# A four-layer diffusion trunk on one core: adaLN chunks spread anew over the stages, and five smaller reorderings

## The chip, the cores and the metric

One Trainium2 chip, one core. The kernel is one launch; its time is the device time of that launch in microseconds, the median of several runs. Every large matrix product is made of three terms of fp32r operands (a value is split in a high and a low part; high x high, high x low and low x high are added up in PSUM).

## The reference, cut to what matters

128 context tokens and 256 latent tokens, 1024 features, four layers. Layer i has the mixer i mod 3: 0 is a gated MLP (gMLP), 1 a pooling mixer, 2 an attention. Each layer ends with a gated convolutional FFN.

```python
def run_trunk(x, cond, is_context, cache_k, cache_v, weights):
    for i in range(DEPTH):                       # 4
        kind, j = i % N_MIXERS, i // N_MIXERS
        sh1, sc1, gt1, sh2, sc2, gt2 = ada_params(cond, w_ada[i], b_ada[i])   # silu(cond) @ w + b
        h = rms_norm(x, g_mix[i]) * (1 + sc1) + sh1
        y = ...                                  # chunk_gmlp, multi_pool or attention
        x = x + gt1 * y
        h = rms_norm(x, g_ffn[i]) * (1 + sc2) + sh2
        x = x + gt2 * conv_ffn(h, w_ffn_in[i], ffn_conv_w[i], ffn_conv_b[i], w_ffn_out[i])

def conv_ffn(h, w_in, conv_w, conv_b, w_out):
    a, u = jnp.split(h @ w_in, 2, axis=-1)       # 2 x 2816
    ap = jnp.pad(a, ((0, 0), (1, 1), (0, 0)))
    a = ap[:, :-2] * conv_w[0] + ap[:, 1:-1] * conv_w[1] + ap[:, 2:] * conv_w[2] + conv_b
    return (jax.nn.gelu(a) * u) @ w_out
```

## The kernel before, in words

**Layout.** Activations lie transposed: 8 tiles (d) of 128 features by 384 tokens in `x`. A product takes a 128x128 block of weights against 384 tokens. Matmuls of the FFN, of the gate half of the gMLP and of the output projections are issued by `mm3` (line 688), those of the first half of the gMLP on line 862, of the pool on line 1030.

**Weights.** All weights come through one stream of 582 chunks, nearly all of 512 KB, in the order of `chunk_plan`, which weaves the adaLN chunks of the table `ADA` into each stage's weights; `EDGES` holds how many weights lead and how many rest. SP issues the loads in that order into five buffers `wraw`; a load waits until the buffer of an earlier chunk is free. A weight chunk is split by ScalarE (`whi`, line 349) and VectorE (`wlo`, line 356) ahead of its use, up to four `wsp` buffers.

**adaLN.** The shift, scale and gate of a layer (six types of 8 chunks each: mixer shift 0, scale 1, gate 2; FFN shift 3, scale 4, gate 5) are products of the conditioning vectors with their own chunks. A chunk "ad" goes to VectorE, `ada_dve`, line 391: two multiply-accumulates, one for each conditioning vector. A chunk "ap" goes to TensorE, `ada_pe`, line 409: eight instruction records in a bank of the pool `psa`; after eight chunks a row copy on ScalarE and, some chunks later, two transposes on TensorE (`ada_fin`). Layer 0's first two types are chunks "a0", two per feature tile, worked on in the start (`a0_mm`, `a0_fin`, `a0_put`), where a hook called after each feature tile's first pass of the first gMLP block finishes tile k+1's scale and shift, norms it, and issues tile k+2's adaLN products. The entries of `ADA` name the layer and stage: gv and gu (first and second half of the gMLP's input), go (its output), fi and fo (FFN input and output), nm, qkv, at (attention's norm, projections and core).

**FFN.** `prep` gives a function `after(d)` that runs behind the residual of tile d (line 464): it scales `x` into `hh` (ScalarE, line 624) and `hl` (VectorE, line 626), and squares x (line 477) into the sum `acc` (line 479; the last square is added later, line 484). The FFN has 22 tiles f, each with a gate half `pa` and a value half `pu`, 48 matmuls a tile. The first `NR` tiles use `hh`, `hl`, which are not yet divided by the rms: these products have two more columns for the shift (386 in all), and their epilogue multiplies by the reciprocal rms (lines 714 to 719). The later tiles use normed inputs, which `put_one` makes in eight steps during tiles 0 to 2, alternately in two forms: for even k, VectorE multiplies (line 585), ScalarE scales (587) and rounds to the high part (588), VectorE subtracts (589); for odd k, VectorE scales and multiplies (592), ScalarE adds the shift into the high part (594), VectorE subtracts (598). Each piece of lines 587, 592, 594 and 598 runs once for the context and once for the latent tokens. PSUM: six banks in the ring `mm`, one in `px` (statistics, transposes), one in `psa`.

**Statistics.** `stats` (line 536) sums `acc`, and a second part where one is given, over the features with matmuls against ones. The pool gives it both `acc` and the last square.

Of the kernel before, what the change touches and what calls it, by code (L numbers as in the profile page):

```python
# [36 lines left out]
NR = 3  # L37
# [243 lines left out]
class Prog:  # L281
# [188 lines left out]
    def square(self, d, acc):  # L470
# [7 lines left out]
        if d < KD - 1:  # L478
            nc.vector.tensor_tensor(out=acc, in0=acc, in1=sq, op=ALU.add)
        return sq  # L480

    def add_square(self, pr):

        self.nc.vector.tensor_tensor(out=pr["acc"], in0=pr["acc"], in1=pr["sq"], op=ALU.add)
# [95 lines left out]
    def put_one(self, k, A, rbs, hi, lo, sh, act):  # L580
# [3 lines left out]
        if act:  # L584
            nc.vector.tensor_tensor(out=t, in0=self.x[:, k, :], in1=rbs, op=ALU.mult)
            for c, (t0, t1) in enumerate(GRPS):
                nc.scalar.activation(t[:, t0:t1], t[:, t0:t1], AF.Identity, scale=A[:, k, c:c + 1], bias=sh[:, k, c:c + 1])
            nc.scalar.activation(hi[:, k, :], t, AF.Copy)
            return lambda: nc.vector.tensor_tensor(out=lo[:, k, :], in0=t, in1=hi[:, k, :].bitcast(F32),
                                                   op=ALU.subtract)  # L590
        for c, (t0, t1) in enumerate(GRPS):
            nc.vector.scalar_tensor_tensor(out=t[:, t0:t1], in0=self.x[:, k, t0:t1], scalar=A[:, k, c:c + 1],
                                           in1=rbs[:, t0:t1], op0=ALU.mult, op1=ALU.mult)
            nc.scalar.activation(hi[:, k, t0:t1], t[:, t0:t1], AF.Identity, bias=sh[:, k, c:c + 1])

        def last():
            for c, (t0, t1) in enumerate(GRPS):
                nc.vector.scalar_tensor_tensor(out=lo[:, k, t0:t1], in0=t[:, t0:t1], scalar=sh[:, k, c:c + 1],
                                               in1=hi[:, k, t0:t1].bitcast(F32), op0=ALU.add, op1=ALU.subtract)
# [1100 lines left out]
```

## Time and profile before

| | us |
|---|---|
| median of 3 runs (lowest to highest) | 1788.74 (1787.39 to 1789.23) |
| the profiled execution's own time | 1788.39 |
| its span, from first to last instruction | 1786.6 |
| mean granted clock of TensorE, of full speed | 0.996 |
| busy: TensorE / VectorE / ScalarE | 1754.6 / 1371.8 / 872.2 |

The profile is one execution. TensorE's busy time counts matmuls whose ends are modelled, weight loads (PEld) overlap them. A line names the source line of the kernel before; the arrow in "out<-in" points from inputs to output. Stages, in us from the span's start: the start to 15, gMLP of layer 0 to 261 with its output stage from about 190, the FFN of layer 0 to 534, pool and FFN of layer 1 to 854 with the output stage from 754, attention from 924 to 971 within layer 2, and the last layer's gMLP and FFN to the end.

### The profile page before, as it was taken

How to read it: one execution, taken by the hardware profiler on the slowest of the kernel's cores; microseconds unless marked ns; L12 is line 12 of the kernel's file. 1: busy time of each engine (PE TensorE's matmuls, PEld its weight loads, DVE VectorE, ACT ScalarE, POOL GpSimd, SP SyncE). 2: the span in 40 equal slices, each digit the busy share in tenths (PEclk: the TensorE clock that was granted, in tenths of full speed). 3: DMA queues.
4: the chain of work that ended last, by engine and by line, in shares of the span. 5: the costliest groups of instructions: out<-in, count | busy, mean ns of one | idle time of the engine just before them, and what ended most of it. 6: DMA issues, size and time to landing. Idle time of an engine off the chain costs nothing.

```text
span 1786.6 us, 26835 instructions
## 1 busy us (share of the span) xinstructions
PE 1754.6 (98%) x10230; PEld 1675.2 (94%) x10230; DVE 1371.8 (77%) x2369; ACT 872.2 (49%) x1635; POOL 1.8 (0%) x30
## 2 busy tenths in 40 slices
PE   9999989999999999999998999999999999999999
PEld 7799889999998899998777999999988999999999
DVE  5888688888986888899687788887775767876632
ACT  3644236545455654432469565453454434755521
POOL 0000000000000000000000000000000000000000
PEclk9999999999999999999999999999999999999999
DMA  8764663555663355567550335655546344354341
GB/s 323 280 222 147 234 211 130 189 191 198 219 212 106 126 181 200 200 214 241 203 183 1 131 130 188 197 176 202 193 150 204 112 145 145 123 175 151 136 150 57
DMA packets 87636, 311.64 MB, mean 174 GB/s; under 512 B 10450, under 2 KB 10962, under 8 KB 87252
## 3 DMA queue, kind: packets, MB, share of 16 engines
q1 hardware_dynamic: 87220, 309.92, 50.9%
q8 instruction: 80, 1.31, 0.3%
q14 instruction: 48, 0.39, 0.1%
q10 hardware_dynamic: 288, 0.01, 0.0%
HBM read 308.06 MB, written 1.84 MB: 173 GB/s over the span
## 4 chain that ended last, share of the span: by engine, by line
PE 61%; DVE 22%; ACT 8%; issue 5%; DMA 4%; SPq 0%; DVEq 0%; ACTq 0%
PE mm L688 45%; DVE wlo L356 7%; DVE junk L391 7%; PE mm L862 6%; DMA wraw<-wts 4%; ACT whi L349 3%; DVE ct L736 3%; PE S L688 1%; PE mm L906 1%; ACT gg L745 1%; DVE gl L606 1%; PE adaT L688 1%; PE S L1138 1%; PE adaT L862 1%; PE psa L862 1%
## 5 line engine op out<-in xcount | busy, mean ns | idle before, releaser
L688 PE MATMUL mm<-hb,whi 128*128 128x384 f32 (+1 forms) x4064 | 888.7, 338 | 6.6 <-ACT whi L349 2.6
L688 PEld LDWEIGHTS mm<-hb,whi 128*128 128x128 f32 x4064 | 722.7, 189 | 11.6 <-ACT whi L349 3.3
L356 DVE TENSOR_TENSOR wlo<-wraw,whi 128x1024 fp32r<-128x1024 f32 (+2 forms) x390 | 466.3, 1201 | 213.7 <-ACT whi L349 212.4
L349 ACT ACTIVATE whi<-wraw 128x1024 fp32r<-128x1024 f32 (+2 forms) x390 | 399.3, 1034 | 270.3 <-PE mm L688 139.4
L688 PE MATMUL mm<-hb,wlo 128*128 128x384 f32 (+1 forms) x2032 | 521.4, 337 | 0.8 <-DVE wlo L356 0.8
L391 DVE SCALAR_TENSOR_TENSOR junk<-wraw,condb 128x1024 bf16<-128x1024 f32 x304 | 371.6, 1222 | 9.1 <-ACT condb L1618 2.7
L688 PEld LDWEIGHTS mm<-hb,wlo 128*128 128x128 f32 x2032 | 369.1, 189 | 1.3 <-DVE wlo L356 1.3
L745 ACT ACTIVATE gg<-ct 128x128 f32<-128x128 f32 (+1 forms) x152 | 47.0, 357 | 248.9 <-DVE ct L736 248.9
L688 PE MATMUL mm<-gh,whi 128*128 128x384 f32 x448 | 123.9, 338 | 3.2 <-ACT whi L349 3.2
L688 PE MATMUL mm<-gh,wlo 128*128 128x384 f32 x448 | 124.2, 338 | 2.4 <-DVE wlo L356 2.4
L688 PE MATMUL mm<-gl,whi 128*128 128x384 f32 x448 | 123.8, 338 | 0.0
L736 DVE SCALAR_TENSOR_TENSOR ct<-ab,par,ct 128x385 f32<-128x385 f32 x176 | 108.7, 619 | 6.4 <-ACT ct L734 2.7
L624 ACT ACTIVATE hb<-x,A 128x128 fp32r<-128x128 f32 x96 | 43.2, 457 | 103.9 <-DVE x L464 93.1
L862 PE MATMUL mm<-whi,hb 128*128 128x512 f32 x320 | 87.6, 399 | 0.0
L688 PEld LDWEIGHTS mm<-gh,whi 128*128 128x128 f32 x448 | 81.9, 189 | 4.1 <-ACT whi L349 4.1
L688 PEld LDWEIGHTS mm<-gh,wlo 128*128 128x128 f32 x448 | 82.0, 189 | 3.6 <-DVE wlo L356 3.6
L688 PEld LDWEIGHTS mm<-gl,whi 128*128 128x128 f32 x448 | 82.3, 189 | 0.0
L746 DVE TENSOR_TENSOR gg<-mm,gg 128x384 f32<-128x384 f32 x76 | 42.4, 558 | 47.4 <-ACT gg L745 46.7
L862 PEld LDWEIGHTS mm<-whi,hb 128*128 128x128 f32 x320 | 60.8, 190 | 15.6 <-ACT hb L573 0.4
L734 ACT ACTIVATE ct<-ab,par 128x385 f32<-128x385 f32 x88 | 62.7, 713 | 3.4
L464 DVE SCALAR_TENSOR_TENSOR x<-mm,prm,x 128x128 f32<-128x128 f32 x92 | 33.6, 411 | 22.9 <-PE mm L688 22.7
L862 PE MATMUL mm<-wlo,hb 128*128 128x512 f32 x160 | 47.8, 405 | 0.0
(286 smaller groups left out, 1651.8 us busy)
## 6 DMA issues: line engine op xcount, KB each, us to landing
wraw<-wts SPq DMA_DIRECT2D x562, 512.0 KB, 3.9
wraw<-wts SPq DMA_DIRECT2D x12, 256.0 KB, 2.6
wraw<-wts SPq DMA_DIRECT2D x8, 384.0 KB, 4.1
x<-x SPq DMA_DIRECT2D x4, 384.0 KB, 4.5
mx<-mix SPq DMA_DIRECT2D x1, 1280.0 KB, 7.8
y<-x SPq DMA_DIRECT2D x3, 384.0 KB, 3.1
condb<-condb SPq DMA_DIRECT2D x1, 1024.0 KB, 7.1
ws<-a_w_s SPq DMA_DIRECT2D x2, 512.0 KB, 4.3
```

The lines of the kernel that those rows point to most:

```text
L349: nc.scalar.activation(hi[:, :n], t[:, :n], AF.Copy)
L356: nc.vector.tensor_tensor(out=lo[:, :n], in0=t[:, :n], in1=hi[:, :n].bitcast(F32), op=ALU.subtract)
L391: nc.vector.scalar_tensor_tensor(out=self.junk.bitcast(BF16), in0=w, scalar=1.0, in1=self.condb[:, c, :], op0=ALU.mult, op1=ALU.mult, accu ...
L464: nc.vector.scalar_tensor_tensor(out=x[:, d, t0:t1], in0=ps[:, t0:t1], scalar=self.prm[:, l, ty * 8 + d, c:c + 1], in1=x[:, d, t0:t1], op0 ...
L606: nc.vector.tensor_tensor(out=lo, in0=src, in1=hi.bitcast(F32), op=ALU.subtract)
L624: nc.scalar.activation(self.hh[:, d, t0:t1], self.x[:, d, t0:t1], AF.Copy, scale=A[:, d, c:c + 1])
L688: nc.tensor.matmul(o, w[:, c:c + nw], r, start=(first and p == 0), stop=(last and p == 2))
L734: nc.scalar.activation(t, ab[:, 1:T + 2], AF.Identity, scale=cw[1], bias=cb)
L736: nc.vector.scalar_tensor_tensor(out=t, in0=ab[:, i:i + T + 1], scalar=cw[i], in1=t, op0=ALU.mult, op1=ALU.add)
L745: nc.scalar.activation(g[:, t0:t1], t[:, t0 + c:t1 + c], GELU)
L746: nc.vector.tensor_tensor(out=g, in0=u, in1=g, op=ALU.mult)
L862: nc.tensor.matmul(ps[n][i], hs, w[p == 1][:, c:c + 512], start=(k == 0 and p == 0), stop=(k == 7 and p == 2))
```

## The change

- `ADA`: the gate half of layer 0's gMLP takes 12 chunks on VectorE instead of 10, its output 9 instead of 12, the input stage of its FFN 19 instead of 18; the input stage of layer 1's FFN 16 instead of 18, its output stage 16 instead of 22. Layer 2's type (2, 3), the FFN's shift, is no longer in layer 1 but goes to TensorE within attention, ahead of (2, 5). Chunks on VectorE are 144 instead of 152, on TensorE 32 instead of 24. In the plan, attention's stage then has ten adaLN chunks, the first two chunks of the output projection, and six adaLN chunks; before, two, the two, and six.
- `NR` is per layer: in layer 1 tile 3 is unnormed too.
- Tile 3 of every FFN takes its two banks from `psa` and `px` instead of the ring.
- `put_one` uses the even form for all eight steps.
- `after(7)` squares first and adds that square to `acc`, ahead of the scaling; the separate additions (lines 773 and 934) go, and the pool's statistic has one part.
- The hook of the first block is called after pass 0 (finish and norm of tile k+1) and again after pass 1 (adaLN products of tile k+2, and the load of `condb`).

```diff
--- before.py
+++ after.py
@@ -34,7 +34,7 @@
 CW = 1024
 TE = T + 2
 
-NR = 3
+NR = (3, 4, 3, 3)
 
 NG = NF - 8
 
@@ -46,15 +46,15 @@
 
 ADA = {
     (0, "gv"): [("ad", 0, 4)],
-    (0, "gu"): [("ad", 0, 2), ("ad", 0, 3, 0, 2)],
-    (0, "go"): [("ad", 0, 3, 2, 8), ("ad", 0, 5, 0, 6), ("ap", 1, 1)],
-    (0, "fi"): [("ad", 0, 5, 6, 8), ("ad", 1, 2), ("ad", 1, 0)],
+    (0, "gu"): [("ad", 0, 2), ("ad", 0, 3, 0, 4)],
+    (0, "go"): [("ad", 0, 3, 4, 8), ("ad", 0, 5, 0, 5), ("ap", 1, 1)],
+    (0, "fi"): [("ad", 0, 5, 5, 8), ("ad", 1, 2), ("ad", 1, 0)],
     (0, "fo"): [("ad", 1, 4), ("ad", 1, 3)],
-    (1, "fi"): [("ad", 1, 5), ("ad", 2, 1), ("ad", 2, 0, 0, 2)],
-    (1, "fo"): [("ad", 2, 0, 2, 8), ("ad", 2, 4), ("ad", 2, 3)],
+    (1, "fi"): [("ad", 1, 5), ("ad", 2, 1)],
+    (1, "fo"): [("ad", 2, 0), ("ad", 2, 4)],
     (2, "nm"): [("ap", 2, 2, 0, 6)],
     (2, "qkv"): [("ap", 2, 2, 6, 8)],
-    (2, "at"): [("ap", 2, 5)],
+    (2, "at"): [("ap", 2, 3), ("ap", 2, 5)],
     (2, "fi"): [("ad", 3, 1), ("ad", 3, 2)],
     (2, "fo"): [("ad", 3, 0), ("ad", 3, 4, 0, 4)],
     (3, "gv"): [("ad", 3, 4, 4, 8), ("ad", 3, 3, 0, 4)],
@@ -467,7 +467,7 @@
         if after is not None:
             after(d)
 
-    def square(self, d, acc):
+    def square(self, d, acc, joined=False):
 
         nc = self.nc
         if d == 0:
@@ -475,13 +475,9 @@
             return None
         sq = self.tmp.tile([128, T], F32, tag="sq", name="sq")
         nc.scalar.activation(sq, self.x[:, d, :], AF.Square)
-        if d < KD - 1:
+        if d < KD - 1 or joined:
             nc.vector.tensor_tensor(out=acc, in0=acc, in1=sq, op=ALU.add)
         return sq
-
-    def add_square(self, pr):
-
-        self.nc.vector.tensor_tensor(out=pr["acc"], in0=pr["acc"], in1=pr["sq"], op=ALU.add)
 
     def new_acc(self):
         return self.tmp.tile([128, T], F32, tag="acc", name="acc", bufs=1)
@@ -577,28 +573,15 @@
                                                scalar=self.prm[:, l, k, c:c + 1], in1=hi[:, k, t0:t1].bitcast(F32),
                                                op0=ALU.add, op1=ALU.subtract)
 
-    def put_one(self, k, A, rbs, hi, lo, sh, act):
+    def put_one(self, k, A, rbs, hi, lo, sh):
 
         nc = self.nc
         t = self.tmp.tile([128, T], F32, tag="sq", name="nt")
-        if act:
-            nc.vector.tensor_tensor(out=t, in0=self.x[:, k, :], in1=rbs, op=ALU.mult)
-            for c, (t0, t1) in enumerate(GRPS):
-                nc.scalar.activation(t[:, t0:t1], t[:, t0:t1], AF.Identity, scale=A[:, k, c:c + 1], bias=sh[:, k, c:c + 1])
-            nc.scalar.activation(hi[:, k, :], t, AF.Copy)
-            return lambda: nc.vector.tensor_tensor(out=lo[:, k, :], in0=t, in1=hi[:, k, :].bitcast(F32),
-                                                   op=ALU.subtract)
+        nc.vector.tensor_tensor(out=t, in0=self.x[:, k, :], in1=rbs, op=ALU.mult)
         for c, (t0, t1) in enumerate(GRPS):
-            nc.vector.scalar_tensor_tensor(out=t[:, t0:t1], in0=self.x[:, k, t0:t1], scalar=A[:, k, c:c + 1],
-                                           in1=rbs[:, t0:t1], op0=ALU.mult, op1=ALU.mult)
-            nc.scalar.activation(hi[:, k, t0:t1], t[:, t0:t1], AF.Identity, bias=sh[:, k, c:c + 1])
-
-        def last():
-            for c, (t0, t1) in enumerate(GRPS):
-                nc.vector.scalar_tensor_tensor(out=lo[:, k, t0:t1], in0=t[:, t0:t1], scalar=sh[:, k, c:c + 1],
-                                               in1=hi[:, k, t0:t1].bitcast(F32), op0=ALU.add, op1=ALU.subtract)
-
-        return last
+            nc.scalar.activation(t[:, t0:t1], t[:, t0:t1], AF.Identity, scale=A[:, k, c:c + 1], bias=sh[:, k, c:c + 1])
+        nc.scalar.activation(hi[:, k, :], t, AF.Copy)
+        return lambda: nc.vector.tensor_tensor(out=lo[:, k, :], in0=t, in1=hi[:, k, :].bitcast(F32), op=ALU.subtract)
 
     def split_act(self, src, hi, lo):
         nc = self.nc
@@ -620,13 +603,16 @@
                 nc.vector.tensor_copy(self.hh[:, :, T:TE], sh)
                 nc.vector.tensor_tensor(out=self.hl[:, :, T:TE], in0=sh, in1=self.hh[:, :, T:TE].bitcast(F32),
                                         op=ALU.subtract)
+            if d == KD - 1:
+                self.square(d, res["acc"], True)
             for c, (t0, t1) in enumerate(GRPS):
                 nc.scalar.activation(self.hh[:, d, t0:t1], self.x[:, d, t0:t1], AF.Copy, scale=A[:, d, c:c + 1])
             for c, (t0, t1) in enumerate(GRPS):
                 nc.vector.scalar_tensor_tensor(out=self.hl[:, d, t0:t1], in0=self.x[:, d, t0:t1],
                                                scalar=A[:, d, c:c + 1], in1=self.hh[:, d, t0:t1].bitcast(F32),
                                                op0=ALU.mult, op1=ALU.subtract)
-            res["sq"] = self.square(d, res["acc"])
+            if d < KD - 1:
+                self.square(d, res["acc"])
             if extra is not None:
                 extra(d)
 
...
@@ -757,7 +743,7 @@
 
                 last = None
                 for k in range(KD):
-                    this = self.put_one(k, pr["A"], rbs, nh, nl, sh, k % 2 == 0)
+                    this = self.put_one(k, pr["A"], rbs, nh, nl, sh)
                     if last is not None:
                         last()
                     last = this
@@ -770,7 +756,6 @@
                 for _ in range(n):
                     next(steps, None)
 
-            self.add_square(pr)
             b = [self.bank()[:, :TE] for _ in range(4)]
             R = None
             for kk in range(4):
@@ -789,8 +774,9 @@
 
             prev = [(0, b[0], b[1]), (1, b[2], b[3])]
             for f in range(2, NF):
-                w0 = TE if f < NR else T
-                pa, pu = self.bank()[:, :w0], self.bank()[:, :w0]
+                w0 = TE if f < NR[l] else T
+
+                pa, pu = (p()[:, :w0] for p in ((self.ps_bank, self.px_bank) if f == 3 else (self.bank, self.bank)))
                 now, prev = (prev, []) if f == 5 else (prev[:1], prev[1:])
                 for kk in range(2):
                     if kk == 0:
@@ -802,11 +788,11 @@
                         w = self.w_get("fi")
                         for st, g in zip(sts, gs):
                             self.split_act(g, gh[st[0]], gl[st[0]])
-                    if f < NR:
+                    if f < NR[l]:
                         norm(3)
                     for k4 in range(4):
                         k = 4 * kk + k4
-                        r = (hh[:, k, :], hl[:, k, :]) if f < NR else (nh[:, k, :], nl[:, k, :])
+                        r = (hh[:, k, :], hl[:, k, :]) if f < NR[l] else (nh[:, k, :], nl[:, k, :])
                         self.mm3([(pa, 256 * k4), (pu, 256 * k4 + 128)], w, r, k == 0, k == 7)
                 prev.append((f, pa, pu))
             assert next(steps, 0) == 0 and len(prev) == 1
@@ -861,8 +847,8 @@
                             hs = (vl if p == 2 else vh)[:, k, 128 * i:128 * i + 128]
                             nc.tensor.matmul(ps[n][i], hs, w[p == 1][:, c:c + 512],
                                              start=(k == 0 and p == 0), stop=(k == 7 and p == 2))
-                    if p == 0 and hook is not None and len(cs) == 2:
-                        hook(k)
+                    if p < 2 and hook is not None and len(cs) == 2:
+                        hook[p](k)
 
             def vout(b, ps):
                 for i in range(3):
@@ -931,7 +917,6 @@
                 vout(1, ps[1])
                 b0, m0 = 2, 0
             else:
-                self.add_square(pr)
                 b = [self.bank()[:, :TE] for _ in range(4)]
                 rbs = None
 
@@ -1060,7 +1045,7 @@
                     aft(d)
 
             first(0)
-            r = self.stats(pr["acc"], pr["sq"])
+            r = self.stats(pr["acc"])
             first(1)
             scaled(0)
             first(2)
@@ -1605,10 +1590,12 @@
         a0_mm(1)
         nc.sync.dma_start(self.cst[:, 0:512], a["cst"][:, 0:512])
 
-        def hook(k):
+        def hook0(k):
             if k + 1 < KD:
                 a0_put(k + 1, a0_fin(k + 1))
-                a0_mm(k + 2)
+
+        def hook1(k):
+            a0_mm(k + 2)
             if k == 3:
                 nc.sync.dma_start(self.condb, a["condb"].rearrange("p (c d) -> p c d", c=2))
             if k == 7:
@@ -1623,7 +1610,7 @@
             kind, j = l % 3, l // 3
             prep = lambda l=l: self.prep(l, 1)
             if l == 0:
-                pr = self.gmlp(l, j, prep, None, hook)
+                pr = self.gmlp(l, j, prep, None, (hook0, hook1))
             elif kind == 0:
                 pr = self.gmlp(l, j, prep, pr)
             elif kind == 1:
```

## Rows read from the trace of the kernel before

**Rows 1.** Page, part 1: busy us (share of the span) and instructions of each engine.
```profile
PE 1754.6 (98%) x10230; PEld 1675.2 (94%) x10230; DVE 1371.8 (77%) x2369; ACT 872.2 (49%) x1635; POOL 1.8 (0%) x30
```

**Rows 2.** Waits of TensorE by releaser, whole span: us in total, times, longest.
```profile
PE mm L688 <- ACT whi L349: 5.7, 4, 2.6
...
PE mm L688 <- DVE wlo L356: 3.2, 5, 0.8
...
PE psa L1550 <- DMA wraw<-wts: 2.7, 3, 1.7
...
PE mm L688 <- DVE hb L589: 2.3, 1, 2.3
...
PE cs L536 <- DVE acc L484: 2.1, 1, 2.1
...
PE mm L688 <- ACT ab L732: 1.0, 2, 0.6
...
PE Tps L1210 <- ACT kd L1205: 0.8, 1, 0.8
```

**Rows 3.** Busy us by stretch: PE, PEld, DVE, ACT, POOL, clock, DMA share, GB/s.
```profile
21.40:24.90 3.50, 3.50 (x10) 2.76 (x9) 1.23 (x1) 1.06 (x1) 0.00 (x0) 0.51 1.04 408
...
247.50:253.50 6.00, 6.00 (x19) 6.00 (x20) 5.90 (x11) 0.00 (x0) 0.00 (x0) 0.50 0.54 183
...
442.50:534.40 91.90, 91.59 (x528) 91.27 (x528) 81.46 (x136) 42.49 (x71) 0.00 (x0) 1.00 0.63 212
...
590.80:620.80 30.00, 26.42 (x147) 24.94 (x145) 24.32 (x43) 18.81 (x38) 0.00 (x0) 1.00 0.33 117
...
754.00:853.90 99.90, 94.64 (x532) 92.54 (x534) 87.68 (x140) 29.61 (x41) 0.00 (x0) 0.98 0.69 234
```

**Rows 4.** Page, parts 5 and 6: groups of instructions; weight chunks with us to landing.
```profile
L356 DVE TENSOR_TENSOR wlo<-wraw,whi 128x1024 fp32r<-128x1024 f32 (+2 forms) x390 | 466.3, 1201 | 213.7 <-ACT whi L349 212.4
...
L391 DVE SCALAR_TENSOR_TENSOR junk<-wraw,condb 128x1024 bf16<-128x1024 f32 x304 | 371.6, 1222 | 9.1 <-ACT condb L1618 2.7
...
wraw<-wts SPq DMA_DIRECT2D x562, 512.0 KB, 3.9
```

**Rows 5.** Timeline of VectorE, gMLP output of layer 0: start, us.
```profile
240.12 1.22 DVE L391 SCALAR_TENSOR_TENSOR junk<-wraw,condb 128x1024 bf16<-128x1024 f32 x1
...
241.27 0.74 DVE L464 SCALAR_TENSOR_TENSOR x<-mm,prm,x 128x128 f32<-128x128 f32 x2
```

**Rows 6.** One line's instructions, lines 409 and 536: ns min/median/max, first and last start.
```profile
L409 PE MATMUL psa<-wraw,cond x192: 379/379/403, 176.9 to 933.4; 128*32 128x256 f32 x192
...
L536 PE MATMUL cs<-ones,sq x12: 250/250/250, 537.4 to 856.5; 128*128 128x1 f32 x12
```

**Rows 7.** Busy time of line 409 alone, end of layer 1.
```profile
853.84:855.27 1.43, 1.43 (x24) 0.67 (x24) 1.00 0.05 19
```

**Rows 8.** Busy time by stretch, attention; the last of three such steps stands.
```profile
938.31:952.09 13.78, 11.28 (x99) 9.65 (x98) 11.20 (x44) 11.22 (x35) 0.00 (x0) 1.00 0.01 2
...
964.77:971.14 6.37, 5.90 (x58) 5.36 (x59) 5.46 (x22) 5.91 (x21) 0.00 (x0) 1.00 0.01 3
```

**Rows 9.** One line's instructions, the norm's lines 585 to 594: ns min/median/max.
```profile
L585 DVE TENSOR_TENSOR nt<-x,rbs x16: 550/556/561, 268.3 to 1528.7; 128x384 f32<-128x384 f32 x16
...
L587 ACT ACTIVATE nt<-nt,prm,A x32: 493/542/590, 268.9 to 1529.7; 128x128 f32<-128x128 f32 x16, 128x256 f32<-128x256 f32 x16
...
L588 ACT ACTIVATE hb<-nt x16: 524/526/527, 269.9 to 1530.3; 128x384 fp32r<-128x384 f32 x16
...
L592 DVE SCALAR_TENSOR_TENSOR nt<-x,A,rbs x32: 345/416/481, 268.8 to 1530.2; 128x128 f32<-128x128 f32 x16, 128x256 f32<-128x256 f32 x16
...
L594 ACT ACTIVATE hb<-nt,prm x32: 384/447/508, 270.4 to 1531.1; 128x128 fp32r<-128x128 f32 x16, 128x256 fp32r<-128x256 f32 x16
```

**Rows 10.** Timelines of VectorE and TensorE, first FFN: last low part, last input used.
```profile
285.75 0.74 DVE L598 SCALAR_TENSOR_TENSOR hb<-nt,prm,hb 128x128 fp32r<-128x128 f32 x2
...
291.10 0.51 PE L688 MATMUL mm<-hb,wlo 128*128 128x384 f32 x2
```

More of the change, by code (lines that the diff above doesn't have):

```diff
@@ L710, in epi_a @@
             def epi_a(f, pa, pu):
-                if f >= NR:
+                if f >= NR[l]:
                     return f, pa, None, pu, None
@@ L742, in epi_c @@
                 g = self.tmp.tile([128, T], F32, tag="gg", name="gg")
-                if f >= NR:
+                if f >= NR[l]:
                     for c, (t0, t1) in enumerate(GRPS):
@@ L804, in ffn @@
                             self.split_act(g, gh[st[0]], gl[st[0]])
-                    if f < NR:
+                    if f < NR[l]:
                         norm(3)
```

## Prediction

> **What bounds the kernel now.** I read the page's engine line first [rows 1]. TensorE is busy for 1754.6 of 1786.6 us, so all its gaps together are 32.0 us; VectorE, busy 1371.8 us, is next. Outside the gaps and the half-clock stretches no faster VectorE or ScalarE can move the end. The reader is to look for two things: where TensorE waits, and where its clock is granted at half.
>
> The waits of TensorE by releaser [rows 2] name few places: a split's high part from ScalarE (5.7 us), its low part from VectorE (3.2), a DMA (2.7), one normed tile (2.3) and the sum of squares (2.1). Then I cut the trace into stages [rows 3]. The pace to compare with is the FFN output stage of layer 0: 528 matmuls in 91.59 busy us, 0.1735 us each. The same stage of layer 1 takes 99.90 us for 532. The remaining windows show half clock (0.50, the 1.2 GHz level) behind the waits, and this nearly doubles what a short wait costs: 247.5 to 253.5 passes 19 matmuls in 6.00 us, which at 0.1735 would be 3.3, so 2.7 us are lost on top of the wait that stands before it.
>
> **The change, part by part.** *Fewer adaLN chunks on VectorE in layer 1's output stage.* A chunk there is two multiply-accumulates of 1.222 us [rows 4], 2.44 us of VectorE, and a split's low part costs 1.20. The stage goes from 22 chunks to 16, which is exactly what layer 0's stage carries. VectorE falls by 6 x 2.44 = 14.7 us, from 87.68 to about 73 of some 92 us; layer 0's is at 81.46 and TensorE is idle there for 91.90 - 91.59 = 0.3 us [rows 3]. Gain: 99.90 - 91.90 - 4 x 0.1735 = 7.3 us; I take 7.2, and 4 to 7.6 as ends (the low end if the wait at the join from the FFN's first half, followed by half clock, survives).
>
> *Second FFN with four unnormed tiles.* In layer 1's FFN TensorE stops once, for 2.3 us, for the normed input that VectorE finishes by line 589 [rows 2]. With tile 3 unnormed the first normed product comes one tile, 48 matmuls, 8.3 us, later; the wait has 6 us to spare. The rest of that stretch holds smaller stops on tiles' epilogues, one on line 732 that keeps a PSUM bank of the ring. The stretch of 30.00 us holds 147 matmuls [rows 3], 25.5 us at pace: 4.5 lost. Tile 3's banks leave the ring, so the bank that line 732 holds is no longer the next one wanted. Added work is two columns of 386 on TensorE and three short VectorE operations. I take 4.4, ends 3.3 and 4.6. The same bank wait elsewhere is half of the row "ab L732" in [rows 2]: another 0.5 us.
>
> *gMLP output and FFN start of layer 0.* VectorE runs four multiply-accumulates of adaLN back to back, the last at 240.12, and only then the residual of output tile 2 at 241.27 [rows 5]; that tile's scaling and square on ScalarE, and the split that TensorE wants next, are queued behind this residual. TensorE's 2.6 us wait for that split, 0.8 for its low part, the 2.7 us of half clock, and 2.1 for the sum of squares add to 8.2 us. The change takes two adaLN chunks away before this residual (4.9 us of VectorE) and one behind it, and puts the last square ahead of the last scaled tile, so line 484's separate addition goes. What replaces a removed chunk's transfer is the next weight, so not all 4.9 us reach TensorE: I take 5.3 of the 8.2, ends 2 and 8.2. The three chunks go to layer 0's gate stage (two) and FFN input (one): 2.44 us each. VectorE is not what TensorE waits for in either stage (no row of [rows 2] falls there), so they are covered; I count +0.5, ends 0 and 3 (a little over one chunk).
>
> *Pool statistics.* The last square is now added by VectorE, so TensorE's six extra records per statistic (250 ns each [rows 6]; the row counts 12, six at this stage) go. Small records overlap: adaLN's go by at 0.06 us each [rows 7]. Six cost between 0.36 and 1.5 us; I take 0.65. The FFN's statistic had one part already.
>
> *The start.* Waiting for the first adaLN chunks costs 1.7 us of TensorE at 20.15 (the longest in the row "DMA" of [rows 2]), and half clock follows: ten matmuls in 3.50 us [rows 3], 1.2 to 1.7 us lost. Splitting the hook puts pass 1's ready matmuls in front of that wait, against one more switch between the two kinds of matmul in six of the steps, which no row prices: nothing, or 0.2 us each if an adaLN record no longer overlaps (0.379 us [rows 6] against the pace of 0.17). SP's issue of condb moves behind pass 1 with it; the first multiply-accumulates on it wait for ScalarE's turn over it [rows 4], off TensorE's path. I take -1.5, ends -3 and +1.2.
>
> *Attention.* Eight more chunks on TensorE, eight records of 379 ns [rows 6] that overlap: 24 of them pass in 1.43 us at the end of layer 1 [rows 7]. A chunk is 0.48 us, eight are 3.8. Three of them fit in the first long window, with 2.5 us of TensorE idle in 13.78 [rows 8]. The later steps have 0.47 us idle in 6.37 and ScalarE is at 5.91 too: the other five cost 2.4 less some 0.5. That is +2.0. The two splits of the first output chunks now fall inside attention: 1.2 us on VectorE each [rows 4] and about as much on ScalarE, where a step leaves VectorE 0.9 and ScalarE 0.5 us [rows 8]; +2.0, ends 0.6 and 2.5. In return the query stage's end loses the split that VectorE put in front of the key's turn, on which TensorE waited 0.8 us ("kd L1205" in [rows 2]). An extra transpose in the output stage is about +0.4 (one chunk's worth, 0.48, as the nearest row). Sum +3.6, ends 0 and 9.
>
> *All eight norm steps through ScalarE.* An odd step cost VectorE four pieces of 0.41 us (1.65) and now two of 0.56 (1.11); ScalarE's two pieces of 0.45 become two of 0.54 and one of 0.53 [rows 9]. Over an FFN: VectorE -2.2 us, ScalarE +2.9. In layer 0 the last low part is ready at 286.49 and the first normed tile comes to that last of its eight inputs at 291.10 [rows 10], so 4.6 us hide ScalarE's 2.9. Priced at nothing; without the cover, it is the rival D. The Trainium skill, "ScalarE: Activation LUTs", section "Rules for kernel authors", would keep additions and multiplications on VectorE; the trace agrees for durations (0.42 against 0.54 for a piece), and by that rule this part would lose 4 x 0.72 = 2.9 us of ScalarE per FFN, but ScalarE is busy for only 49% of the span.
>
> The sum: -7.2 - 4.4 - 0.5 - 5.3 + 0.5 - 0.65 - 1.5 + 3.6 = -15.45 us. Against the profiled execution's own 1788.39 that is 1772.9; the median of the runs is 0.35 above it. Predicted: 1773.0 us.
>
> **The rivals.** *A: attention takes it back.* The two output splits hold loads behind them, so the last three adaLN chunks are awaited there. One landing takes 3.9 us [rows 4] and SP issues in plan order; two such waits are 7.8 us, with the half clock of 2.7 behind one 10.5: 1781 to 1783.5. For it: ScalarE and VectorE are both within 0.5 to 0.9 us of the step's length. Against: only 16 chunks are asked of a stage that moves almost no bytes today (DMA share 0.01).
>
> *B: VectorE's backlog only moves.* Layer 0's late residual and layer 1's stage keep their waits because the freed VectorE time pulls the next chunk's multiply-accumulate forward and the weight behind it lands no sooner. Then 5.3 falls to 2, 7.2 to 4, and the gate stage costs 3: 9.0 us less gain, 1782.
>
> *C: the gain is off the path.* TensorE's waits are replaced by waits for loads: -4.9 (layer 1's FFN and the bank) against +3.6 leaves about -1: 1787.
>
> *D: slower, by the norm on ScalarE.* Two buffers carry the norm's steps, so if step k+2 must wait for step k's low part, each step is a chain of 0.56 + 2 x 0.54 + 0.53 + 0.56 = 2.7 us; fully in series 8 steps are 21.8 us against VectorE's 11.0 now. The delay of 10.8 less the 4.6 us of cover stops the first normed tile for 6.2 us, and half clock adds 2.7: 8.9 in each of layers 0, 2 and 3, 26.7 us, less the 15.45: 1799.6. It decides once the norm loses more than 4.6 us in an FFN. Against: two buffers allow two steps in flight, and the steps are handed out between tiles at a pace that VectorE's queue already stretches. If that chain is half overlapped, as today, it costs nothing.
>
> *After the waits: the clock.* Half clock (0.50) follows the waits of 2.6 and 1.7 us [rows 2, 3], and not the 2.3 us on line 589: its stretch has 1.00 [rows 3]. So the clock's part of the gain is uncertain by 2.7 + 1.5 us. It stands in the ends. The Trainium skill, "TensorE: Matmul & The Clock Gate", section "HAM oscillation", says idle gaps between groups throttle the engine again; the trace agrees with the 0.50 rows, and this gap stayed without one.
>
> **How the numbers follow.** Forecast 0.68 (1766 to 1779), A 0.12, B 0.11, C 0.04, D 0.05. All good ends together give -24.6, all bad ends +2.8. They will not come together: I go three quarters of the way to the good ones, -22.3 (1766), since waits that are seen in rows stand behind them, and a third to the bad ones, -9.4 (1779). To hold 8 in 10 the range takes in A and most of B: 1766 to 1783. A measurement of this kernel tells about 0.2%, 3.6 us, from no change: the bound is 1785.1. Faster: the forecast, A and B, 0.91, less 0.02 for B's worst: 0.89. Within 0.2%: C and that rest, 0.06. Slower: D, 0.05.
>
> **What the profile would show.** Right: the wait on line 589 gone and the 147 matmuls at 590 to 621 in about 25.6 us; layer 1's output stage near 92 us with VectorE near 73; no half clock near 250 and 770; TensorE's attention steps about 0.5 us longer where a chunk was added. Wrong: half clock inside attention or a wait for "wraw" there (A); the same waits on whi and wlo at the ends of the output stages (B); a wait on lines 588 or 589 in layers 0, 2 or 3 (D). A faster start shows as the 0.50 stretch at 21.4 gone or shorter, and no DMA wait on line 1550 there. The forecast is wrong by more than its range if attention grows by over 12 us, or if layer 0's and layer 1's output stages both keep their length.

## The result: 0.9917 of the time before, and the profile after

The changed kernel takes 1773.99 us (median of 4 runs, 1773.20 to 1775.46) against 1788.99: a ratio of 0.9917, interval 0.9900 to 0.9934. Run again it gave 0.9922 (0.9907 to 0.9937). Forecast: 1773.0 in 1766 to 1783. The profiled execution took 1774.25, its span is 1772.5.

Page, part 1 and part 4 of the kernel after, to be read against [rows 1]:

```profile
PE 1753.0 (99%) x10290; PEld 1669.9 (94%) x10290; DVE 1347.4 (76%) x2309; ACT 883.1 (50%) x1653; POOL 1.8 (0%) x30
...
PE 78%; DVE 13%; ACT 5%; issue 3%; DMA 1%; SPq 0%; DVEq 0%; ACTq 0%
```

TensorE's gaps fell from 32.0 us to 19.5. Waits of TensorE in the kernel after, whole span, against [rows 2] (lines moved: 688 is now 674, 589 is 584, 536 is 532):

```profile
PE mm L674 <- DVE wlo L356: 5.5, 8, 1.0
PE psa L1535 <- DMA wraw<-wts: 1.8, 3, 0.7
...
PE cs L532 <- DVE acc L479: 0.8, 1, 0.8
```

The waits on high parts, on the normed tile, on the banks and on the key's turn are gone. The row of low parts grew, from 3.2 us in five waits to 5.5 in eight, and that of a transpose in attention ("DVE aes") from 0.2 to 0.9. Busy us by stretch in the kernel after (columns as in [rows 3]): the start, the join from gMLP output to FFN in layer 0, layer 1's FFN input where the old wait was, layer 1's output stage.

```profile
18.00:24.90 6.90, 6.20 (x40) 4.20 (x40) 4.57 (x10) 1.97 (x3) 0.00 (x0) 1.00 0.92 347
239.00:252.00 13.00, 12.24 (x72) 11.96 (x70) 11.30 (x20) 6.58 (x11) 0.27 (x6) 1.00 0.52 171
584.05:613.90 29.85, 28.11 (x160) 27.48 (x159) 22.49 (x39) 19.08 (x35) 0.00 (x0) 1.00 0.34 116
747.20:838.65 91.45, 91.45 (x532) 91.20 (x534) 72.41 (x112) 29.64 (x40) 0.00 (x0) 1.00 0.64 214
```

No stretch within the span is at half clock any more. The output stage passes its 532 matmuls in 91.45 us without a gap, with VectorE at 72.41 (forecast: near 92, near 73). The third row is the surprise: TensorE still has 1.7 us of gaps there.

**Where the time went.** The two traces hold the same 8952 matmuls on split weights, in the same order, so each can be matched. I took the start of one matmul at each seam between stages in both traces; the difference of the differences is what a stage gained (minus) or lost. The columns to the right are experiments, all against the trace before, told below. One profiled execution each.

| stage (us in the trace before) | forecast | changed | newada | oldada | altnorm_timed | oldbank | at_back |
|---|---|---|---|---|---|---|---|
| start, to 57.4 | -1.5 | -1.78 | +0.75 | -2.25 | -2.48 | -2.61 | -2.46 |
| gate half, to 200.1 | +0.5 with the FFN input | +0.78 | +0.80 | +0.02 | +0.79 | +0.79 | +0.78 |
| gMLP output, FFN start, to 261.8 | -5.3 | -8.23 | -8.46 | -1.32 | -8.38 | -9.22 | -8.65 |
| FFN 0 input, to 440.1 | -0.5 (bank) | +2.76 | +1.22 | +3.25 | +1.20 | +2.73 | +2.75 |
| FFN 0 output, to 530.1 | 0 | +0.40 | +0.46 | +0.28 | +0.40 | +0.39 | +0.65 |
| pool, to 548.3 | -0.65 | -0.68 | 0 | -0.68 | -0.68 | -0.68 | -0.68 |
| FFN 1 input, to 760.0 | -4.4 | -0.05 | -0.82 | +2.29 | -1.75 | +2.37 | -0.05 |
| FFN 1 output, to 850.1 | -7.2 | -8.45 | -8.45 | +3.45 | -8.45 | -8.45 | +4.42 |
| query stage, to 914.1 | -0.8 | -1.17 | -1.12 | -0.01 | -1.15 | -1.15 | +0.01 |
| attention and its output, to 992.0 | +4.4 | +2.25 | +2.26 | -0.06 | +2.27 | +2.24 | -0.01 |
| the rest, to 1780 | 0 | +0.03 | +0.03 | +0.02 | +0.03 | +2.99 | +0.02 |
| sum | -15.45 | -14.14 | -13.33 | +4.99 | -18.20 | -10.60 | -3.22 |

The sum was right to 1.3 us; single terms were not. Layer 0's join and layer 1's output gave 4.2 us more than forecast, attention with the query stage cost 2.5 less, and both FFN input stages together cost 2.7 us where 4.9 were to be gained. Stages that did better than forecast by 7.0 us in sum and stages that did worse by 8.3 nearly cancel: that the total came so close is luck.

### The profile page after: what moved, and what is told of

It is laid out like the page before. It is cut to its first block, busy times and chain, and to the rows that moved or that the text cites. A ratio compares the mean times of both kernels' runs of the same rounds, so it can differ in the third digit from the quotient of the medians.

```text
span 1772.5 us, 26883 instructions
## 1 busy us (share of the span) xinstructions
PE 1753.0 (99%) x10290; PEld 1669.9 (94%) x10290; DVE 1347.4 (76%) x2309; ACT 883.1 (50%) x1653; POOL 1.8 (0%) x30
## 4 chain that ended last, share of the span: by engine, by line
PE 78%; DVE 13%; ACT 5%; issue 3%; DMA 1%; SPq 0%; DVEq 0%; ACTq 0%
PE mm L674 59%; PE mm L848 6%; DVE wlo L356 4%; DVE junk L391 4%; ACT whi L349 2%; DVE ct L722 2%; DMA wraw<-wts 1%; PE S L674 1%; PE adaT L674 1%; PE mm L892 1%; PE psa L674 1%; PE S L1123 1%; PE adaT L848 1%; PE psa L848 1%; PE mm L1015 1%
## 5 line engine op out<-in xcount | busy, mean ns | idle before, releaser
L674 PE MATMUL mm<-hb,whi 128*128 128x384 f32 (+1 forms) x3936 | 858.8, 337 | 0.0
L674 PEld LDWEIGHTS mm<-hb,whi 128*128 128x128 f32 x3936 | 697.8, 188 | 3.5 <-issue 1.2
L674 PE MATMUL mm<-hb,wlo 128*128 128x384 f32 (+1 forms) x1968 | 504.7, 337 | 4.9 <-DVE wlo L356 4.9
L674 PEld LDWEIGHTS mm<-hb,wlo 128*128 128x128 f32 x1968 | 356.0, 188 | 7.7 <-DVE wlo L356 7.7
L391 DVE SCALAR_TENSOR_TENSOR junk<-wraw,condb 128x1024 bf16<-128x1024 f32 x288 | 351.9, 1222 | 7.9 <-ACT condb L1605 2.7
```

What stands on the lines that cost most here:

```text
L391: nc.vector.scalar_tensor_tensor(out=self.junk.bitcast(BF16), in0=w, scalar=1.0, in1=self.condb[:, c, :], op0=ALU.mult, op1=ALU.mult, accu ...
L674: nc.tensor.matmul(o, w[:, c:c + nw], r, start=(first and p == 0), stop=(last and p == 2))
```

## The experiments

**The table alone, and all but the table.**

```diff
 newada: before.py with the new ADA;  oldada: after.py with
-    (0, "gu"): [("ad", 0, 2), ("ad", 0, 3, 0, 4)],
+    (0, "gu"): [("ad", 0, 2), ("ad", 0, 3, 0, 2)],
...
+    (1, "fo"): [("ad", 2, 0, 2, 8), ("ad", 2, 4), ("ad", 2, 3)],
```

> Edit: the kernel before with the new ADA table alone. Theory (the table carries most of the gain, by layer 0's gMLP output and layer 1's FFN output): against before, gMLP output and FFN start of layer 0 -7 us, layer 0's FFN +2.5 (new waits on low parts), layer 1's FFN input stage about 0 or a little worse (the 2.3 us norm wait stays), layer 1's output stage -8.4, query stage -1.1, attention +2.2, gate stage +0.8: about -10.5, 1778 us. Rival (the table moves VectorE's backlog and the gain needs the smaller edits with it): within 4 us of before, 1785 or more.

> Edit: the changed kernel with the old ADA table. Theory (the table carries the two big terms): layer 0's gMLP output loses about 8 us again less some 1 us of the earlier square, layer 1's output stage 8.4; the start keeps -1.8, the pool -0.8; layer 1's FFN input stage is 4.3 us shorter than before, since with the old places of the adaLN chunks the low parts are not late: about 1781 us. Rival (late low parts in layer 1's FFN come from the fourth unnormed tile or the norm on ScalarE, not from the table): layer 1's FFN input stage as in the changed kernel, 0 to 0.5 us shorter than before: 1785 us.

Measured: newada 1775.06 us, oldada 1793.38 (one run each), before beside them 1787.02 (median of 9). The table alone brings 13.33 of the 14.14 us, more than I expected. The other edits without it make the kernel slower, by 5.0 us in the trace. Neither theory had that. In layer 0's join newada gains 8.46 us, as much as the whole change: the earlier last square, which newada lacks, adds nothing that the trace shows. Waits of TensorE in oldada, and busy us of its join in layer 0 and the end of its output stage in layer 1:

```profile
PE mm L674 <- DVE wlo L356: 7.3, 10, 1.2
PE mm L674 <- ACT whi L349: 6.5, 6, 1.8
PE cs L532 <- DVE acc L479: 3.1, 1, 3.1
...
250.00:264.00 14.00, 10.93 (x46) 10.64 (x46) 9.53 (x19) 6.50 (x11) 0.00 (x0) 0.76 0.68 221
...
843.90:850.70 6.80, 6.11 (x19) 6.12 (x20) 6.08 (x11) 1.85 (x4) 0.00 (x0) 0.50 0.53 172
```

With the old table all the waits on the two split halves stand as before, and longer, and half clock comes with them. It covers some 20 us of oldada's trace in four stretches (at 257, 612, 772 and 844 us), some 13.5 us of the trace before in three. Half of such a stretch is lost, so by my estimate about 3.3 of the 5.0 us are the clock's, and a single execution does not show how often they come. The gains of table and edits don't add in these traces: -13.33 and +4.99 against -14.14 for both. Which of the edits costs most under the old table was not run.

**Is it the place of an adaLN chunk within a tile?** In the changed kernel the new chunk counts put layer 1's chunks, from tile 5 to 12, behind the first weight of each tile, between its two splits; before, the chunks of tiles 4 to 11 stood behind the second.

```diff
-EDGES = {(0, "gv"): (2, 1), ...
+EDGES = {(1, "fi"): (8, 4), (0, "gv"): (2, 1), ...          # slots1
+EDGES = {(1, "fi"): (8, 4), (0, "fi"): (8, 0), (0, "gv"): (2, 1), ...          # slots2, and
-    (0, "go"): [..., ("ad", 0, 5, 0, 5), ...],   (0, "fi"): [("ad", 0, 5, 5, 8), ...
+    (0, "go"): [..., ("ad", 0, 5, 0, 6), ...],   (0, "fi"): [("ad", 0, 5, 6, 8), ...
```

> Edit: the changed kernel, the 16 adaLN chunks of layer 1's FFN input stage one weight earlier, so that each stands behind a tile's second weight instead of the first (EDGES of that stage 8, 4 instead of 8, 2). Same work, same stage. Theory (an adaLN chunk between a tile's first split and its epilogue makes the second low part late by about 1 us): the waits on low parts between 597 and 634 us go, -4 us, 1770 us. Rival (VectorE simply has too much work in that stretch with four unnormed tiles, or ScalarE with the norm): the waits stay in number and size, 1774 us.

> Edit: slots1, and in layer 0 one adaLN chunk back from the FFN input stage to the gMLP's output (18 and 10 chunks), with the FFN input's 18 chunks behind the second weight of every tile from 4 to 21. Theory (places decide): layer 0's FFN loses its waits on low parts too, -3 us, and the gMLP's output gives back 0 to 2.4 us (one chunk's VectorE time): 1768 to 1771 us. Rival (amount decides: VectorE's backlog at the gMLP's end comes back with the tenth chunk, with half clock behind it): +4 to 6 there, 1772 us or more.

Measured: slots1 1775.97 us (ratio 0.9936, 0.9921 to 0.9951), slots2 1778.96 (0.9950, 0.9938 to 0.9963; its trace is of the fastest of five executions, 1775.91). The theory falls for layer 1. TensorE's waits between 580 and 640 us, first in the kernel after, then in slots1:

```profile
PE mm L674 <- DVE wlo L356: 3.1, 4, 1.0
```

```profile
PE mm L674 <- DVE wlo L356: 2.9, 4, 1.0
PE mm L674 <- ACT whi L349: 2.1, 2, 1.1
```

The low parts are as late as in the changed kernel, and two waits on high parts come on top (that the first chunk, now one weight earlier, causes them is not shown). The newada run speaks against places too: it has the same places as the changed kernel and no such waits. In slots2 layer 0's FFN input goes from +2.76 to +0.82 in the table's terms, with one chunk fewer; that confounds place and amount. For layer 0 they stay confounded: best1 and best2 below also take a chunk out, and with 18 chunks the plan puts them back in the places of before.

**Which of the edits makes the low parts late?**

```diff
 nr3:
-NR = (3, 4, 3, 3)
+NR = (3, 3, 3, 3)
 altnorm: put_one of before.py, and
-                    this = self.put_one(k, pr["A"], rbs, nh, nl, sh)
+                    this = self.put_one(k, pr["A"], rbs, nh, nl, sh, k % 2 == 0)
 oldbank:
-                pa, pu = (p()[:, :w0] for p in ((self.ps_bank, self.px_bank) if f == 3 else (self.bank, self.bank)))
+                pa, pu = (p()[:, :w0] for p in ((self.ps_bank, self.px_bank) if f == 99 else (self.bank, self.bank)))
```

> Edit: the changed kernel with three unnormed tiles in layer 1 as elsewhere. The new table alone left no waits on low parts between 597 and 634 us, the whole change has five there (4 us). Theory (the fourth unnormed tile's epilogue is the VectorE work that makes the low parts late): these waits go, -4 us, and the wait for the normed input comes back, +2.3 us, and +2.9 if half clock follows it as it did with the new table alone: within 2 us of the changed kernel. Rivals (norm on ScalarE, or the banks outside the ring): the low parts stay late and the norm's wait is added: 2.3 to 5 us slower than the changed kernel.

> Edit: the changed kernel with the old two forms of the norm's steps in turn. Theory (the norm on ScalarE is covered and costs nothing): layers 2 and 3 as in the changed kernel within 0.3 us, layer 0's wait on a low part at 308 us and layer 1's five stay: same time. Rival (ScalarE's 2.9 us per FFN delay its splits): the wait at 308 us goes (-0.9 us) and most of the five in layer 1 (-2 to -4 us).

> Edit: the changed kernel with tile 3's banks in the ring again in every FFN. Theory (outside the ring tile 3 only moves a wait): in layer 0 a bank wait of about 0.5 us returns near 300 us and the 0.9 us on a low part right behind it goes, sum 0 to -0.4; in layer 1 a bank wait of about 0.6 returns per release and the waits on low parts shrink by as much: within 1 us of the changed kernel. Rival (the banks are a gain of their own): 1 to 2 us slower.

Measured: 1775.22, 1770.03 and 1777.80 us (one run each). The waits of which the first two expectations count five, 4 us, are the four of 3.1 us shown above. The norm on ScalarE is not free. With the old two forms layer 0's FFN input loses 1.20 us instead of 2.76, and layer 1's gains 1.75 instead of 0.05. The rows show how. ScalarE in layer 1's FFN of the kernel after:

```profile
585.56 0.97 ACT L582 ACTIVATE nt<-nt,prm,A 128x128 f32<-128x128 f32 x2
586.56 0.53 ACT L583 ACTIVATE hb<-nt 128x384 fp32r<-128x384 f32 x1
587.00 0.97 ACT L582 ACTIVATE nt<-nt,prm,A 128x128 f32<-128x128 f32 x2
588.00 0.52 ACT L583 ACTIVATE hb<-nt 128x384 fp32r<-128x384 f32 x1
588.53 1.28 ACT L734 ACT_TABLE_LOAD   x1
589.82 0.53 ACT L734 ACTIVATE ct<-ct 128x385 f32<-128x385 f32 x1
590.25 1.04 ACT L349 ACTIVATE whi<-wraw 128x1024 fp32r<-128x1024 f32 x1
```

Norm steps stand back to back, 1.44 us each, ahead of a tile's epilogue and of the next split. VectorE and TensorE a little later in the same trace:

```profile
595.11 0.56 DVE L584 TENSOR_TENSOR hb<-nt,hb 128x384 fp32r<-128x384 f32 x1 [1.15 <-ACT hb L583]
...
596.43 0.56 DVE L705 TENSOR_TENSOR u<-mm,rbs 128x384 f32<-128x384 f32 x1 [0.30 <-ACT be L703]
596.91 1.22 DVE L356 TENSOR_TENSOR wlo<-wraw,whi 128x1024 fp32r<-128x1024 f32 x1
```

```profile
598.18 0.62 PE L674 MATMUL mm<-hb,wlo 128*128 128x384 f32 x2 [0.98 <-DVE wlo L356]
607.55 0.62 PE L674 MATMUL mm<-hb,wlo 128*128 128x384 f32 x2 [0.75 <-DVE wlo L356]
616.84 0.63 PE L674 MATMUL mm<-hb,wlo 128*128 128x384 f32 x2 [0.70 <-DVE wlo L356]
622.08 0.61 PE L674 MATMUL mm<-hb,wlo 128*128 128x384 f32 x2 [0.64 <-DVE wlo L356]
```

At the first of these four waits VectorE does not lack time, it waits for ScalarE (1.15 us for a high part of the norm) and reaches the split late, just ahead of TensorE. The releaser that the wait names, VectorE, is only the last link. The norm is not the whole cause: with the old forms (altnorm_timed below) three waits on low parts, 1.6 us, are left in this stretch. The Trainium skill, "ScalarE: Activation LUTs", section "Rules for kernel authors", would keep additions and multiplications on VectorE; here the run bears the sign out for layers 0 and 1 (1.56 and 1.70 us), while layers 2 and 3 show no difference (-18.23 at 992 and -18.20 at the end with the old forms, -14.17 and -14.14 with the new).

The fourth unnormed tile is worth little. In nr3 the norm's wait comes back, TensorE's waits between 580 and 640 being now:

```profile
PE psa L674 <- DVE hb L584: 2.9, 1, 2.9
PE psa L674 <- ACT hb L583: 0.5, 1, 0.5
```

and half clock behind it (588 to 600 us at 0.86). Yet that stage ends 0.5 us later only than in the changed kernel (+0.49 against -0.05), since all four waits on low parts are gone. Removing TensorE's stop did not make the stage shorter. The reading that fits these runs is that the stop had been the time in which ScalarE and VectorE caught up, and that they take it back tile by tile.

In layers 2 and 3 tile 3's banks are more than a moved wait, against what I expected. In oldbank TensorE waits for line 703, which reads the shift's columns out of a tile's bank behind ScalarE's norm steps, in every FFN; the first row is from its waits, the second from its timeline in layer 1:

```profile
PE mm L674 <- ACT be L703: 5.9, 4, 3.7
...
594.53 1.41 PE L674 MATMUL mm<-hb,whi 128*128 128x384 f32 x2 [3.71 <-ACT be L703]
```

Layers 2 and 3 lose 1.5 us each (+2.99 in the table's last row but one), layer 1 2.4, and layer 0 nothing (+2.73 against +2.76). Layer 1's 2.4 us hold a stretch at half clock behind the wait of 3.71 us, from 594 to 601 us: 19 matmuls in 6.75 us, by estimate some 3 us over the pace of 0.1735, so one trace does not show what the banks are worth there without it. In the trace before, where the norm took turns, there is no such wait in layers 2 and 3. So in those layers the bank edit buys back what the norm edit would cost, and the pair gains nothing.

**The norm's price, timed, and two versions that go on from it.**

```diff
 best1: altnorm, and
-    (0, "fi"): [("ad", 0, 5, 5, 8), ("ad", 1, 2), ("ad", 1, 0)],
-    (0, "fo"): [("ad", 1, 4), ("ad", 1, 3)],
+    (0, "fi"): [("ad", 0, 5, 5, 8), ("ad", 1, 2), ("ad", 1, 0, 0, 7)],
+    (0, "fo"): [("ad", 1, 0, 7, 8), ("ad", 1, 4), ("ad", 1, 3)],
 best2: altnorm, and
-    (0, "gu"): [("ad", 0, 2), ("ad", 0, 3, 0, 4)],
-    (0, "go"): [("ad", 0, 3, 4, 8), ("ad", 0, 5, 0, 5), ("ap", 1, 1)],
-    (0, "fi"): [("ad", 0, 5, 5, 8), ("ad", 1, 2), ("ad", 1, 0)],
+    (0, "gu"): [("ad", 0, 2), ("ad", 0, 3, 0, 5)],
+    (0, "go"): [("ad", 0, 3, 5, 8), ("ad", 0, 5, 0, 6), ("ap", 1, 1)],
+    (0, "fi"): [("ad", 0, 5, 6, 8), ("ad", 1, 2), ("ad", 1, 0)],
```

> Edit: none, the changed kernel again, beside the two below on the same chip. Every theory: 0.990 to 0.9934 of before, as first measured.

> Edit: the changed kernel with the old two forms of the norm's steps in turn, timed. Theory (ScalarE's longer norm is not covered in layers 0 and 1; there it delays the splits and the epilogue): 3 to 4 us under the changed kernel. Rival (the 4 us of the first look were mostly the chance of the start and of the sum of squares' wait, 1.5 us): 1.5 us or less under it.

> Edit: altnorm, and one adaLN chunk moved from layer 0's FFN input stage (19, now 18, in the places of before) to its output stage (16, now 17). Theory (the 19th chunk, with two chunks in one tile at 12, makes the low parts late at 357, 424 and 446 us): these three waits go, -2.3 us against altnorm, and the output stage, whose VectorE has 10 us spare, hides its chunk: 1768 us where altnorm is 1770. Rival (VectorE's backlog at the seam moves into the output stage): 0.3 to 0.8 us are given back there at its first waits: about 1770.

> Edit: altnorm, and one adaLN chunk fewer in layer 0's FFN input stage (18), moved up through the output stage (9 as before, other chunks) into the gate half (13 instead of 12). Theory (VectorE, which waits 3.2 us for TensorE at the end of that stage and 6.6 us for ScalarE's splits in it, has room for one more chunk there, while the FFN input stage has not): -2.4 us in the FFN input, 0 to +0.8 in the gate half: 1768 us, about 2 under altnorm. Rival (every stage of layer 0 up to the pool is full, and a chunk costs its 2.4 us of VectorE wherever it stands): no gain, 1770 us.

Measured:

| | us, median (range) | ratio to before, interval |
|---|---|---|
| again | 1773.33 (1772.26 to 1774.27) | 0.9922 (0.9907 to 0.9937) |
| altnorm_timed | 1770.31 (1769.87 to 1772.07) | 0.9908 (0.9891 to 0.9925) |
| best1 | 1771.66 (1770.00 to 1771.80) | 0.9911 (0.9896 to 0.9925) |
| best2 | 1770.66 (1768.99 to 1771.90) | 0.9895 (0.9881 to 0.9909) |

The kernel with the old norm is 3.0 us under the changed kernel on the same chip, and the ranges don't overlap; the traces say 3.1 (-18.20 against -15.07 for again). It beats both kernels. Of the 4 us between the first traces 1 us was luck at the start (-1.78 in the changed kernel's first trace, -2.74 in again).

Both attempts to free layer 0's FFN input of its 19th chunk remove its three waits on low parts (-2.4 us) and pay them back elsewhere. TensorE's waits between 260 and 540 us in altnorm_timed, in best1, and between 100 and 540 in best2:

```profile
PE mm L687 <- DVE wlo L356: 1.8, 3, 0.6
```

```profile
PE mm L687 <- DVE wlo L356: 0.8, 1, 0.8
PE mm L687 <- ACT whi L349: 0.8, 1, 0.8
```

```profile
PE mm L905 <- DVE ct L912: 1.7, 5, 0.6
```

best1 gives 2.1 back at 513 us, at the end of the output stage; best2 gives 2.5 back in the gate half (135 to 156 us), on the gate's products. There VectorE is busy 37.39 of 40 us:

```profile
120.00:160.00 40.00, 38.29 (x231) 36.86 (x230) 37.39 (x61) 13.74 (x23) 0.00 (x0) 1.00 0.60 199
```

This is best2's rival: the chunk in question costs about its 2.4 us of VectorE in each of the three stages of layer 0 in which it was tried. It holds for the last chunk put in, not for every one: the two that the change itself moved into the gate half cost 0.78 us there together, and the next one 2.5. The idle rows on which the theory rested (waits of VectorE for TensorE and for ScalarE) lay behind that place, where they could not be used.

**Attention against the output stage.**

```diff
 at_back:
-    (1, "fo"): [("ad", 2, 0), ("ad", 2, 4)],
+    (1, "fo"): [("ad", 2, 0), ("ad", 2, 4), ("ad", 2, 3)],
-    (2, "at"): [("ap", 2, 3), ("ap", 2, 5)],
+    (2, "at"): [("ap", 2, 5)],
```

> Edit: the changed kernel with layer 2's FFN shift back on VectorE in layer 1's output stage (24 chunks there instead of 16) and out of attention. Theory (22 chunks cost that stage 8.4 us, attention pays 2.25 for eight, the query stage gains 1.1 by the later output splits): output stage +8.4 to +13, query stage +1.1, attention -2.2: 1781 to 1786 us. Rival (the stage's waits came from the backlog that layer 1's input stage handed over, not from its own chunks): the output stage grows by less than 4 us: 1777 us or less.

Measured: 1785.19 us (one run), as the theory had it. The output stage of at_back:

```profile
752.30:850.10 97.80, 90.67 (x492) 87.73 (x491) 85.99 (x137) 26.59 (x34) 0.00 (x0) 0.97 0.71 233
```

It is 12.9 us longer than in the changed kernel (+4.42 against -8.45), 1.6 us for each of the eight chunks, with VectorE at 85.99 of 97.80 in the stretch shown. Two stretches of 3.4 us at half clock (at 812 and 843 us) are part of it; half of them, some 3.4 us by my estimate, is lost to the clock. Attention and the query stage return to their old length, 1.08 us shorter in sum than in the changed kernel. So the exchange of eight chunks is 12.9 us for 1.1, without any backlog handed over: the FFN input stage ahead of it is the same in both to 0.01 us.

## Why the prediction was right, point by point

*The stages with too many chunks on VectorE.* Right in kind, too low in size. Layer 1's output gave 8.45 for 7.2, and VectorE is at 72.41 for the forecast 73; the low end, a surviving wait at the join, did not come. Layer 0's join gave 8.23 for 5.3, all that the four listed losses held, and newada's 8.46 says that the table alone does it. The reserve (removed transfers are replaced by weights) was not needed. In the trace after, four multiply-accumulates still run ahead of that residual, but it stands 6.4 us earlier than in [rows 5]:

```profile
234.90 0.74 DVE L464 SCALAR_TENSOR_TENSOR x<-mm,prm,x 128x128 f32<-128x128 f32 x2
```

Two chunks are 4.9 us of VectorE, and 1.0 was gained by then (the table's first two rows). Rival B fell.

*The fourth unnormed tile: a term that failed.* It was to gain 4.4 us and the stage gained 0.05. The wait on line 589 went as said (-2.3), and the small waits on epilogues and banks too (-1.3); between 580 and 640 us of the trace before they were:

```profile
PE mm L688 <- ACT ab L732: 0.6, 1, 0.6
PE mm L688 <- DVE u L719: 0.5, 2, 0.3
PE mm L688 <- ACT be L716: 0.2, 1, 0.2
```

But 3.1 us came back as four waits on low parts that the sum did not hold, and TensorE is busy 0.4 us longer in the stage. The small waits are gone in newada as well, whose tiles and banks are those of before, so they went with the table. What I named as the sign, "about 25.6 us for the 147 matmuls", shows the failure in part: 29.85 us for 160, 27.8 at pace; two of the four waits lie behind that window. The step "the wait has 6 us to spare" looked at the one input only. It did not ask what TensorE's stop had been worth to the engines that feed it.

*The norm on ScalarE, priced at nothing: mis-sized by 3.1 us.* I had the term (ScalarE +2.9 us per FFN) and gave it the slack of the last normed input. The slack was there, and no normed input was late in layers 0, 2 and 3. But ScalarE's queue also holds the epilogues and the splits, and these had less. Rival D named the right engine and the wrong wait; its price of 26.7 us did not come, 3.1 did, in layers 0 and 1.

*The displaced chunks.* Gate half +0.78, within the ends. FFN input of layer 0: with the old norm the stage loses 1.20, and taking away its 19th chunk, which also moves the others back to their places of before, gains 2.4 by the output stage, one chunk's whole VectorE time. "They are covered", since no wait stood there before, was wrong: no wait only said that VectorE had kept up with the chunks it had. With the old norm the bank's 0.5 us came as forecast (best2: -0.48 for the stage).

*Pool, start.* -0.68 for -0.65. The start -1.78 for -1.5, up to -2.74 in other runs of the same code there (again); in newada, without the split hook, it is +0.75, and its longest DMA wait is 2.0 us where the changed kernel has 0.7.

*Attention.* +1.08 for +3.6. The query stage gave 1.17, the eight chunks cost 2.25 in all: the two output splits, for which I took 2.0, cannot have cost that beside the chunks' own 2.0. Part of the chunks' time filled waits: of TensorE's waits for ScalarE within attention, "ACT T" at line 1237 (now 1222) fell from 1.5 to 0.3 us and "ACT P" at 1259 (now 1244) from 1.2 to 0.3. A single trace does not split the 2.25 further. Rival A fell: there is no wait for a weight's landing in attention.

*Rival C* had the right mechanism for a part of the gain (waits replaced by others) and the wrong engine.

*The arithmetic.* -15.45 and the 0.35 make 1773.3, not 1773.0; nothing hangs on it.

## What to carry over

A stop of the bound engine can also be the time in which the engines that feed it catch up; before its removal is counted as a gain, sum what they have to do in the stretch up to the next wait. That no wait stands in a stage does not show how much room is left in it: layer 0's gate half took two more chunks for 0.78 us together and the third for 2.5, while attention, where TensorE stood idle for 2.5 us of one window, took eight as TensorE's work for a net 1.1 us. An engine's slack is that of the earliest thing in its queue, not that of the instruction that was changed.

## What the runs showed of the hardware that I had not expected

Half clock is not tied to the length of one wait. In the trace before, a wait of 2.26 us at 600 is followed by full clock; in newada a wait of 2.25 us at the same matmul is followed by half clock. The wait, and busy us of 3.3 us behind it, before and newada:

```profile
600.13 0.98 PE L688 MATMUL mm<-hb,whi 128*128 128x384 f32 x4 [2.26 <-DVE hb L589]
...
600.10:603.40 3.30, 3.04 (x16) 2.75 (x17) 3.00 (x6) 2.73 (x7) 0.00 (x0) 1.00 0.32 123
```

```profile
594.89 1.55 PE L688 MATMUL mm<-hb,whi 128*128 128x384 f32 x4 [2.25 <-DVE hb L589]
...
595.10:598.40 3.30, 3.30 (x11) 3.30 (x11) 3.00 (x5) 2.47 (x6) 0.00 (x0) 0.50 0.25 101
```

16 matmuls in one, 11 in the other: at the forecast's pace of 0.1735 us about 1.4 us were lost, an estimate. In nr3 half clock comes in the query stage, where no wait is longer than 0.9 us; the stage takes 1.7 us more there (+0.51 against the changed kernel's -1.17), although nr3's edit is in another stage:

```profile
842.90:849.60 6.70, 5.83 (x15) 3.61 (x12) 4.58 (x10) 3.49 (x6) 0.00 (x0) 0.50 0.78 320
```

So a wait's price carries an uncertainty of its own, here 1.4 us behind this wait and 2.7 behind that at 246 us in the trace before, which I could not read off the trace before. The Trainium skill, "TensorE: Matmul & The Clock Gate", section "HAM oscillation", says that idle gaps throttle the engine again; newada's row agrees, the row before shows an equal gap that did not.
